# A recurrence's output bank: last part of the first four chunks behind the next chunk's first burst, and one ScalarE copy out of the bank

## The chip, the cores and the metric

The kernel runs on one core of a Trainium2 chip. The metric is the time of one execution in microseconds of the device. TensorE (PE) multiplies matrices into the accumulation banks (PSUM), VectorE (DVE), ScalarE (ACT) and GpSimd (POOL) work on tiles, SyncE (SP) issues most transfers. A bank holds 512 fp32 values for each of 128 partitions.

## The reference

One decoder layer for 2048 tokens of width 1024. The normed input is projected once and the result cut into three branches, each with a gate: a sliding-window attention, a cross-attention into 256 memory tokens, and a recurrence with a state matrix for each of 8 heads of width 64. The change touches only the recurrence:

```python
def rwkv7_scan(r, w, k, v, a, b):
    def step(S, inp):
        r_t, w_t, k_t, v_t, a_t, b_t = inp
        sa = jnp.einsum('bhvk,bhk->bhv', S, a_t)
        S = S * w_t[:, :, None, :] + sa[..., None] * b_t[:, :, None, :] + v_t[..., None] * k_t[:, :, None, :]
        y = jnp.einsum('bhvk,bhk->bhv', S, r_t)
        return S, y
...
    y = rwkv7_scan(rh, heads(decay), kh, vh, -kk, kk * ah)
    mean = jnp.mean(y, axis=-1, keepdims=True)
    var = jnp.mean(jnp.square(y - mean), axis=-1, keepdims=True)
    y = ((y - mean) * lax.rsqrt(var + LNX_EPS)).reshape(bsz, t, RW_WIDTH) * lnx_g.astype(f32) + lnx_b.astype(f32)
```

The three gated branches are projected, merged and added to the input.

## The kernel before

The tokens are worked through in four blocks of 512. In a block two streams are written side by side: `stream_r`, the recurrence, and `stream_f`, the two attentions and their projections. A projection (`proj`, through `gemm3`, L457 to L459) is 24 dense matmuls of 128x512 in the rounded fp32 format, since each operand is split into a high and a low part. Its result lies in one of two banks called mm, from which ACT or DVE takes it; `silu2` (L927 a tanh on ACT, L928 a product on DVE) is such a reader.

The recurrence takes its eight heads as four pairs, and the pairs in two groups of two. For a group, `rwkv_prep` makes the scaled keys and queries of all chunks of 64 tokens (QE and QO; AB; BK: L728 to L743 on DVE, L753 and L770 on PE, where L770 transposes BK), `rwkv_inverse` inverts a triangular matrix for each chunk, and `rwkv_chain` goes through the eight chunks in order. So a block has two chains, and the kernel eight. For chunk `c` a chain runs these bursts, four small fp32 matmuls each (two for S), each of which the profile shows as two passes:

- W (L866): state and values into a bank, copied to SBUF by DVE (L869).
- the w-part (L867): the chunk's first part of the output, into the bank `yps`. It reads what W reads.
- U (L874): the inverse times W; DVE multiplies the result into Z (L878, two products).
- the u-part (L859, `from_u`): the second part of the output. It needs the products of L878. For chunk `c` it is written behind U of chunk `c+1`, but for the chunks 3 and 7 into a burst of its own (L886).
- S (L881): the state's update; DVE adds it (L882) to the decayed state that ACT prepared (L872), and the next W needs that.

W and the w-part work on tiles of 128x64, U and the u-part on 64x64, S on the full 128x128.

The bank `yps` exists once and holds the output of four chunks, so a chain fills it twice. After chunk 3 and after chunk 7 DVE reads the bank: a sum over each head (L889), its mean (L890), and two subtractions into SBUF (L894). Only then may the w-part of chunk 4 open the bank again. Behind the chain come the variance (L900 on ACT, L902 on DVE), the scaling (L907) and four transposes (L910).

The order of instructions on each engine is not that of the program: `order` hands the whole program to a list scheduler (`steps`, `lay_out`) which goes by modelled durations (`cost_PE`, `cost_DVE` and so on) and by ranks, and the result is pinned for each engine. `burst` makes its matmuls one group that starts when all its operands are there (`together`); `behind` only fixes an order on PE. What a step of the recurrence waits for, PE fills with dense matmuls of projections. The temporary tiles of the recurrence come from `tmp`, six in turn.

Of the kernel before, what the change touches and what calls it, by code (L numbers as in the profile page):

```python
# [9 lines left out]
F32 = mybir.dt.float32  # L10
# [17 lines left out]
C = 64  # L28
NC_ = TB // C
# [268 lines left out]
def build(tc, A, nsb=4):  # L298
# [27 lines left out]
    def rw_ps():  # L326
        return ps.tile([128, 512], F32, name="rw", bufs=2)
# [509 lines left out]
    def rwkv_chain(group, Z, dk, hT, yas):  # L837
# [6 lines left out]
        def burst(ms, prev=None, after=()):  # L844
            together(ms)
            for m in ms:
                for u in after:
                    behind(m, u, True)
                if prev:
                    behind(m, prev)  # L850
                after, prev = (), m
            return prev
# [7 lines left out]

        upds = []
        for c in range(NC_):
            if c % per == 0:
                yps = y_ps().rearrange("p (i t e v) -> p i t e v", i=n, t=per // 2, e=2)
            pw = rw_ps()[:, :n * C].rearrange("p (i t) -> p i t", i=n)
            prev = burst([PE.matmul(pw[h, i], g[1][e][:, c, :C], Z[:, i, e, c], start=True, stop=True) for i, e, h, g in HH], None, upds)  # L866
            burst([PE.matmul(yslot(i, c, e), g[1][e][:, c, C:], Z[:, i, e, c], start=i == 0 and c % per == 0, stop=False) for i, e, h, g in HH], prev)  # L867
            W = rp.tile([128, n, C], F32, name="W", bufs=1)
            V.tensor_copy(W, pw)  # L869
# [5 lines left out]
            if c % per:  # L875
                prev = burst(from_u(c - 1), prev)
# [8 lines left out]
            if c % per == per - 1:  # L885
                burst(from_u(c), prev, upds[:1])  # L886

                mean = xp.tile([128, 8], F32, name="st8", bufs=2)
                V.tensor_reduce(mean, yps.rearrange("p i t e v -> p (i t e) v"), axis=AX.X, op=ALU.add)  # L889
                V.tensor_scalar(mean, mean, 1.0 / C, None, op0=ALU.mult)  # L890
                for i in range(n):
                    if c < per:
                        ycs.append(tmp())
                    V.tensor_tensor(chunks(ycs[i])[:, c // per * per:(c // per + 1) * per], yps[:, i].rearrange("p t e v -> p (t e) v"),  # L894
                                    mean[:, i * per:(i + 1) * per].unsqueeze(2).to_broadcast([128, per, C]), op=ALU.subtract)

# [482 lines left out]
```

## Time and profile before

| | |
|---|---|
| median of 3 runs | 2250.22 us (2249.85 to 2250.74) |
| the profiled execution | 2250.33 us |
| its span, first to last instruction | 2248.5 us |
| mean granted TensorE clock | 0.997 |
| dense matmuls of the projections on PE, `hH` and `hL` (L457 to L459) | 5664, 2248.0 us of overlapping durations |
| one dense matmul, duration in the record | 397 ns |

A matmul's duration in the record overlaps with that of the next, so its cost to PE is read from the distance of two starts. The rows of the timeline give start and length in us, engine, line, operation, what is written and what is read, and in brackets how long the engine sat idle before it and for whom. Groups of instructions give busy time in us and mean ns of one.

### The profile page before, as it was taken

To read this page: it belongs to the slowest core of one execution; us is meant where nothing else is said; L and a number is where in the kernel's file an instruction comes from. 1 tells how busy PE (TensorE), PEld (TensorE's weight loads), DVE (VectorE), ACT (ScalarE), POOL (GpSimd) and SP (SyncE) were. 2 spreads that over 40 slices of the span, in tenths; PEclk is the share of its full clock that TensorE was granted. 3 is DMA by queue.
4 is the path that set the end of the run, shared out by engine and by line. 5 is a ranking of instruction groups with operands and counts; after the bars stand their busy time and mean duration, and the time that the engine had idled before them with its cause. 6 is when DMAs were issued, how large, how long until landed. Compare 5 with 4: busy or idle time off the path is not lost.

```text
span 2248.5 us, 36875 instructions
## 1 busy us (share of the span) xinstructions
PE 2219.2 (99%) x13706; PEld 1806.1 (80%) x13706; DVE 1533.0 (68%) x3951; ACT 926.2 (41%) x2024; POOL 147.9 (7%) x209
## 2 busy tenths in 40 slices
PE   8999999999999999999999999999999999999999
PEld 7888778778888778878888878787888887787887
DVE  7799789775469777953437957985245895896312
ACT  6664565455253354423214345442223435434210
POOL 1000110000000011000000001000000001100000
PEclk9999999999999999999999999999999999999999
DMA  7777546679844444446774434445676444343655
GB/s 230 265 234 241 195 164 226 231 264 356 323 146 161 134 141 149 147 166 234 241 239 136 164 122 150 148 136 194 229 252 198 157 141 160 117 146 132 206 192 192
DMA packets 146226, 430.55 MB, mean 191 GB/s; under 512 B 16640, under 2 KB 21120, under 8 KB 146048
## 3 DMA queue, kind: packets, MB, share of 16 engines
q1 hardware_dynamic: 129920, 398.83, 52.6%
q10 hardware_dynamic: 16128, 29.37, 4.0%
q8 instruction: 109, 1.79, 0.3%
q14 instruction: 69, 0.57, 0.1%
HBM read 333.24 MB, written 94.90 MB: 190 GB/s over the span
## 4 chain that ended last, share of the span: by engine, by line
PE 74%; DVE 18%; ACT 3%; DMA 2%; issue 2%; POOL 1%; SPq 0%; DVEq 0%; ACTq 0%; POOLq 0%
PE mm L457 18%; PE mm L459 18%; PE mm L458 18%; DVE ibc L803 1%; PE rw L881 1%; DVE ibc L804 1%; ACT g L1102 1%; DVE Yi L805 1%; PE mm L1172 1%; PE mm L1174 1%; PE mm L1173 1%; PE oo L1003 1%; PE rw L866 1%; PE rw L874 1%; DVE g L1114 1%
## 5 line engine op out<-in xcount | busy, mean ns | idle before, releaser
L457 PE MATMUL mm<-hH,whl 128*128 128x512 f32 x1888 | 750.4, 397 | 5.8 <-DVE g L928 3.5
L459 PE MATMUL mm<-hH,whl 128*128 128x512 f32 x1888 | 748.9, 397 | 0.0
L458 PE MATMUL mm<-hL,whl 128*128 128x512 f32 x1888 | 748.7, 397 | 0.0
L457 PEld LDWEIGHTS mm<-hH,whl 128*128 128x128 f32 x1888 | 355.1, 188 | 77.9 <-DVE g L928 3.9
L459 PEld LDWEIGHTS mm<-hH,whl 128*128 128x128 f32 x1888 | 355.3, 188 | 69.4
L458 PEld LDWEIGHTS mm<-hL,whl 128*128 128x128 f32 x1888 | 355.3, 188 | 68.3 <-issue 0.7
L439 ACT ACTIVATE whl<-raw 128x512 fp32r<-128x512 f32 x178 | 111.2, 629 | 146.9 <-PE mm L459 80.1
L440 DVE TENSOR_TENSOR whl<-raw,whl 128x512 fp32r<-128x512 f32 x178 | 124.5, 702 | 50.6 <-ACT whl L439 49.5
L457 PE MATMUL mm<-yh,whl 128*128 128x512 f32 x384 | 151.3, 394 | 0.0
L458 PE MATMUL mm<-yl,whl 128*128 128x512 f32 x384 | 150.8, 393 | 0.0
L459 PE MATMUL mm<-yh,whl 128*128 128x512 f32 x384 | 150.7, 393 | 0.0
L872 ACT ACTIVATE SP<-Z,Pl 64x64 f32<-64x64 f32 x256 | 88.3, 345 | 115.0 <-DVE Z L882 111.4
L803 DVE STREAM_SHUFFLE ibc<-Nc 128x496 f32<-128x496 f32 (+30 forms) x248 | 113.4, 473 | 0.1
L1155 DVE SCALAR_TENSOR_TENSOR g<-g,mm 128x512 f32<-128x512 f32 x32 | 21.8, 681 | 128.6 <-PE mm L459 128.5
L804 DVE TENSOR_TENSOR ibc<-ibc,Yi 128x496 f32<-128x496 f32 (+30 forms) x248 | 104.5, 421 | 3.9
L805 DVE TENSOR_TENSOR Yi<-Yi,ibc 128x496 f32<-128x496 f32 (+30 forms) x248 | 103.2, 416 | 0.9
L882 DVE SCALAR_TENSOR_TENSOR Z<-rw,Pl,SP 64x64 f32<-64x64 f32 x224 | 63.5, 284 | 51.1 <-PE rw L881 47.5
L1140 ACT ACTIVATE gt<-mm 128x512 f32<-128x512 f32 x64 | 38.0, 593 | 144.1 <-PE mm L459 143.8
L457 PEld LDWEIGHTS mm<-yh,whl 128*128 128x128 f32 x384 | 72.1, 188 | 15.0 <-DVE g L1155 0.4
L459 PEld LDWEIGHTS mm<-yh,whl 128*128 128x128 f32 x384 | 72.1, 188 | 14.6
L458 PEld LDWEIGHTS mm<-yl,whl 128*128 128x128 f32 x384 | 72.1, 188 | 14.3
L1102 ACT ACTIVATE g<-g,mxs,st 128x256 f32<-128x256 f32 (+1 forms) x128 | 74.5, 584 | 18.4 <-DVE mxs L1095 18.2
(1902 smaller groups left out, 3783.9 us busy)
## 6 DMA issues: line engine op xcount, KB each, us to landing
whl<-k SPq DMA_DIRECT2D x486, 512.0 KB, 3.3
k<-whl SPq DMA_DIRECT2D x162, 512.0 KB, 4.4
raw<-in_w_in SPq DMA_DIRECT2D x118, 256.0 KB, 3.3
g<-in_x ACTq DMA_DIRECT2D x32, 256.0 KB, 4.4
out<-g ACTq DMA_DIRECT2D x32, 256.0 KB, 4.5
raw<-in_w_proj SPq DMA_DIRECT2D x24, 256.0 KB, 3.1
rt<-in_x ACTq DMA_DIRECT2D x24, 256.0 KB, 5.7
rt<-in_xt ACTq DMA_DIRECT2D x24, 256.0 KB, 5.8
```

The source lines that it names most:

```text
L439: S.activation(w[:, 0], raw, AF.Copy)
L440: V.tensor_tensor(w[:, 1], raw, w[:, 0].bitcast(F32), op=ALU.subtract)
L457: PE.matmul(out, lh, rh, start=i == 0, stop=False)
L458: PE.matmul(out, lh, rl, start=False, stop=False)
L459: PE.matmul(out, ll, rh, start=False, stop=i == n - 1)
L803: V.stream_shuffle(bc[:, :, :w], N_[:, :, s + 1:], [s] * 32)
L804: V.tensor_tensor(bc[:, :, :w], bc[:, :, :w], Y[:, :, s:s + 1].to_broadcast([128, n, w]), op=ALU.mult)
L805: V.tensor_tensor(Y[:, :, s + 1:], Y[:, :, s + 1:], bc[:, :, :w], op=ALU.add)
L872: S.activation(SP[h, i], Z[h, i, e, c], AF.Copy, scale=g[4][h, c:c + 1])
L882: upds = [V.scalar_tensor_tensor(Sst[h, g[0]] if c == NC_ - 1 else Z[h, i, e, c + 1], pS[h, i, e], g[4][h, c:c + 1], SP[h, i], op0=ALU.mul ...
L1102: S.activation(prs[b][:, i, m0:], prs[b][:, i, m0:], AF.Exp, scale=r2[:, b, i:i + 1], bias=mx[:, b, i:i + 1], accum_out=mx[:, b, 2 + i:3 + i])
L1140: S.activation(t, gp, AF.Tanh, scale=0.5)
```

## The change

The bank is taken out by one copy of ACT into a temporary tile (`take_y`, L868 of the new kernel); sum, mean and subtractions read that tile (L871 to L876), and one more tile of six is in use meanwhile. The u-part of chunk 3 is written behind W of chunk 4 (a burst of its own no more), the bank is emptied there, and the w-part of chunk 4 (`from_w`, L863) is written behind U of chunk 4, in the place where other chunks have a u-part; S stands behind it. The chain's end has the copy as well, with its u-part where it was. Nothing else is edited, but the scheduler lays out the program anew.

```diff
@@ -858,21 +858,47 @@
 
             return [PE.matmul(yslot(i, c, e), g[2][h, c, C:], Z[h, i, e, c], start=False, stop=i == n - 1 and c % per == per - 1) for i, e, h, g in HH]
 
+        def from_w(c):
+
+            return [PE.matmul(yslot(i, c, e), g[1][e][:, c, C:], Z[:, i, e, c], start=i == 0 and c % per == 0, stop=False) for i, e, h, g in HH]
+
+        def take_y(last):
+
+            full = tmp()
+            S.activation(full, yps.rearrange("p i t e v -> p (i t e v)"), AF.Copy)
+            part = full.rearrange("p (i s v) -> p i s v", i=n, v=C)
+            mean = xp.tile([128, 8], F32, name="st8", bufs=2)
+            V.tensor_reduce(mean, part.rearrange("p i s v -> p (i s) v"), axis=AX.X, op=ALU.add)
+            V.tensor_scalar(mean, mean, 1.0 / C, None, op0=ALU.mult)
+            for i in range(n):
+                if last < per:
+                    ycs.append(tmp())
+                V.tensor_tensor(chunks(ycs[i])[:, last // per * per:(last // per + 1) * per], part[:, i],
+                                mean[:, i * per:(i + 1) * per].unsqueeze(2).to_broadcast([128, per, C]), op=ALU.subtract)
+
         upds = []
         for c in range(NC_):
+            later = c % per == 0 and c
+            pw = rw_ps()[:, :n * C].rearrange("p (i t) -> p i t", i=n)
+            prev = burst([PE.matmul(pw[h, i], g[1][e][:, c, :C], Z[:, i, e, c], start=True, stop=True) for i, e, h, g in HH], None, upds)
+            if later:
+                burst(from_u(c - 1), prev)
+            W = rp.tile([128, n, C], F32, name="W", bufs=1)
+            V.tensor_copy(W, pw)
+            if later:
+                take_y(c - 1)
             if c % per == 0:
                 yps = y_ps().rearrange("p (i t e v) -> p i t e v", i=n, t=per // 2, e=2)
-            pw = rw_ps()[:, :n * C].rearrange("p (i t) -> p i t", i=n)
-            prev = burst([PE.matmul(pw[h, i], g[1][e][:, c, :C], Z[:, i, e, c], start=True, stop=True) for i, e, h, g in HH], None, upds)
-            burst([PE.matmul(yslot(i, c, e), g[1][e][:, c, C:], Z[:, i, e, c], start=i == 0 and c % per == 0, stop=False) for i, e, h, g in HH], prev)
-            W = rp.tile([128, n, C], F32, name="W", bufs=1)
-            V.tensor_copy(W, pw)
+            if not later:
+                burst(from_w(c), prev)
             SP = rp.tile([128, n, C], F32, name="SP", bufs=1)
             for i, e, h, g in HH:
                 S.activation(SP[h, i], Z[h, i, e, c], AF.Copy, scale=g[4][h, c:c + 1])
             pu = rw_ps()[:, :n * C].rearrange("p (i t) -> p i t", i=n)
             prev = burst([PE.matmul(pu[h, i], g[2][h, c, :C], W[h, i], start=True, stop=True) for i, e, h, g in HH])
-            if c % per:
+            if later:
+                prev = burst(from_w(c), prev)
+            elif c:
                 prev = burst(from_u(c - 1), prev)
             for e, h in ((0, EV), (1, OD)):
                 upd = V.tensor_tensor(Z[h, :n, e, c], pu[h], dk[h, :n, c:c + 1].to_broadcast([64, n, C]), op=ALU.mult)
@@ -882,18 +908,8 @@
             upds = [V.scalar_tensor_tensor(Sst[h, g[0]] if c == NC_ - 1 else Z[h, i, e, c + 1], pS[h, i, e], g[4][h, c:c + 1], SP[h, i], op0=ALU.mult, op1=ALU.add)
                     for i, e, h, g in HH]
             yield 4.247
-            if c % per == per - 1:
-                burst(from_u(c), prev, upds[:1])
-
-                mean = xp.tile([128, 8], F32, name="st8", bufs=2)
-                V.tensor_reduce(mean, yps.rearrange("p i t e v -> p (i t e) v"), axis=AX.X, op=ALU.add)
-                V.tensor_scalar(mean, mean, 1.0 / C, None, op0=ALU.mult)
-                for i in range(n):
-                    if c < per:
-                        ycs.append(tmp())
-                    V.tensor_tensor(chunks(ycs[i])[:, c // per * per:(c // per + 1) * per], yps[:, i].rearrange("p t e v -> p (t e) v"),
-                                    mean[:, i * per:(i + 1) * per].unsqueeze(2).to_broadcast([128, per, C]), op=ALU.subtract)
-
+        burst(from_u(NC_ - 1), prev, upds[:1])
+        take_y(NC_ - 1)
 
         for (p, _, _, _, _, yt), yc in zip(group, ycs):
             ysq = tmp()
```

Three places of the order. The first is PE at the boundary between the fourth and the fifth chunk, second group of the second block (mm are projections, rw the banks of W and U). Before, where the u-part of the fourth chunk stands alone two dense matmuls ahead of these rows, and four dense ones and S follow them:

```order
L866 MATMUL rw<-Z,QE 64x64
L866 MATMUL rw<-Z,QO 64x64
L866 MATMUL rw<-Z,whl 64x64 x2
L459 MATMUL mm<-hH,whl 128x512
L457 MATMUL mm<-yh,whl 128x512
L458 MATMUL mm<-yl,whl 128x512
L459 MATMUL mm<-yh,whl 128x512
L874 MATMUL rw<-W,AB 64x64 x2
L874 MATMUL rw<-W,whl 64x64 x2
L867 MATMUL yps<-Z,QE 64x64
L867 MATMUL yps<-Z,QO 64x64
L867 MATMUL yps<-Z,whl 64x64 x2
```

And after, where seven dense matmuls are ahead of the rows, and six and S follow (L883 is W, L859 the u-part, L898 U, L863 the w-part):

```order
L883 MATMUL rw<-Z,QE 64x64
L883 MATMUL rw<-Z,QO 64x64
L883 MATMUL rw<-Z,whl 64x64 x2
L859 MATMUL yps<-Z,AB 64x64 x2
L859 MATMUL yps<-Z,whl 64x64 x2
L457 MATMUL mm<-yh,whl 128x512
L898 MATMUL rw<-W,AB 64x64 x2
L898 MATMUL rw<-W,whl 64x64 x2
L458 MATMUL mm<-yl,whl 128x512
L863 MATMUL yps<-Z,QE 64x64
L863 MATMUL yps<-Z,QO 64x64
L863 MATMUL yps<-Z,whl 64x64 x2
```

The u-part joined W, and the w-part left U: one dense matmul now stands between them. In the first group of a block it is two.

The second place is PE in the same block's second preparation, where the keys BK are transposed into a bank of rw. Before:

```order
L457 MATMUL mm<-hH,whl 128x512
L458 MATMUL mm<-hL,whl 128x512
L770 MATMUL rw<-c_ident,BK 128x128 x4
L459 MATMUL mm<-hH,whl 128x512
L770 MATMUL rw<-c_ident,BK 128x128 x4
```

After:

```order
L459 MATMUL mm<-hH,whl 128x512
L457 MATMUL mm<-hH,whl 128x512
L770 MATMUL rw<-c_ident,BK 128x128 x8
L458 MATMUL mm<-hL,whl 128x512
L459 MATMUL mm<-hH,whl 128x512
```

Two stretches of transposes became one.

The third place is DVE in the first block, in the preparation of the second group, just behind the first chain's end. A projection's matmul on PE waits for the silu product there (L928, and L944 after), since it opens the bank that the product reads. Before:

```order
L728 SCALAR_TENSOR_TENSOR QO<-rt,Pt 64x8x64
L730 SCALAR_TENSOR_TENSOR rt<-rt 128x512
L735 TENSOR_TENSOR rk__2989<-rk__2989,rt 128x512
L440 TENSOR_TENSOR whl<-raw,whl 128x512
L732 TENSOR_TENSOR BK<-rt 64x8x64
L742 TENSOR_TENSOR QE<-rr__3114,Pt 64x8x64
L732 TENSOR_TENSOR BK<-rt 64x8x64
L440 TENSOR_TENSOR whl<-raw,whl 128x512
L928 SCALAR_TENSOR_TENSOR g_3505<-g_3505,mm 128x512
L737 TENSOR_TENSOR BK<-rk__2989,rt 64x8x64 x2
L742 TENSOR_TENSOR QO<-rr__3114,Pt 64x8x64
```

After:

```order
L730 SCALAR_TENSOR_TENSOR rt<-rt 128x512
L735 TENSOR_TENSOR rk__2993<-rk__2993,rt 128x512
L732 TENSOR_TENSOR BK<-rt 64x8x64
L440 TENSOR_TENSOR whl<-raw,whl 128x512
L732 TENSOR_TENSOR BK<-rt 64x8x64
L737 TENSOR_TENSOR BK<-rk__2993,rt 64x8x64 x2
L742 TENSOR_TENSOR QE<-rr__3118,Pt 64x8x64
L440 TENSOR_TENSOR whl<-raw,whl 128x512
L944 SCALAR_TENSOR_TENSOR g_3509<-g_3509,mm 128x512
L742 TENSOR_TENSOR QO<-rr__3118,Pt 64x8x64
```

The two products of L737 moved from behind the silu product to ahead of it. An instruction of the window attention (the one of L1094, three rows behind the silu product before) moved ahead of it too, further up.

## Prediction

> **What bounds the kernel now.** I read the engine table first, then the chain of work that ended last, then what TensorE (PE) waited for.
>
> ```profile
> PE 2219.2 (99%) x13706; PEld 1806.1 (80%) x13706; DVE 1533.0 (68%) x3951; ACT 926.2 (41%) x2024; POOL 147.9 (7%) x209
> PE 74%; DVE 18%; ACT 3%; DMA 2%; issue 2%; POOL 1%; SPq 0%; DVEq 0%; ACTq 0%; POOLq 0%
> PE mm L457 <- DVE g L928: 3.5, 1, 3.5
> PE rw L866 <- DVE Z L882: 2.4, 4, 1.4
> PE rw L881 <- DVE Z L878: 1.1, 3, 0.4
> ```
>
> PE has work for 99% of the span and carries 74% of the chain; it has almost always a projection to run while the recurrence waits for VectorE (DVE). So an edit pays in two ways only: by what PE itself spends, or by one of the few waits in the last three rows (us in total, times, longest). A shorter or longer recurrence by itself is worth nothing while projections fill the gap. The profiled execution took 2250.33 us (span 2248.5, 1.8 outside it), against a median of 2250.22; I sum against 2250.33 and take off 0.1 at the end.
>
> What a small burst costs PE is read around the boundary between the fourth and the fifth chunk, here that of the second group in the second block of tokens. I call the bursts by their lines: W (L866), its y part (L867, "w-part"), U (L874), the part from u (L859, "u-part") and S (L881). Between them stand dense 128x512 matmuls.
>
> ```profile
> 972.73 0.39 PE L459 MATMUL mm<-hH,whl 128*128 128x512 f32 x1
> ...
> 974.10 0.39 PE L459 MATMUL mm<-hH,whl 128*128 128x512 f32 x1
> 974.42 0.27 PE L866 MATMUL rw<-Z,QE 128*64 128x64 f32 x1
> ...
> 975.37 0.40 PE L458 MATMUL mm<-hL,whl 128*128 128x512 f32 x1
> 975.69 0.33 PE L874 MATMUL rw<-W,AB 64*64 64x64 f32 x4
> ...
> 976.64 0.39 PE L457 MATMUL mm<-hH,whl 128*128 128x512 f32 x1
> ```
>
> Six dense matmuls take 974.10 - 972.73 = 1.37, so 0.228 each. I count a stretch of small matmuls as the time from the start of the dense one before it to the start of the second dense one behind it, less two times 0.228: that takes in the slower slots on both sides. W with its w-part: 975.37 - 974.10 - 0.46 = 0.81. U with the u-part: 976.64 - 975.37 - 0.46 = 0.81.
>
> ```profile
> 978.23 0.40 PE L459 MATMUL mm<-hH,whl 128*128 128x512 f32 x1
> 978.56 0.33 PE L859 MATMUL yps<-Z,AB 64*64 64x64 f32 x4
> ...
> 979.27 0.40 PE L458 MATMUL mm<-hL,whl 128*128 128x512 f32 x1
> 979.60 0.27 PE L866 MATMUL rw<-Z,QE 128*64 128x64 f32 x1
> ...
> 980.32 0.39 PE L457 MATMUL mm<-yh,whl 128*128 128x512 f32 x1
> ...
> 980.79 0.39 PE L459 MATMUL mm<-yh,whl 128*128 128x512 f32 x1
> 981.11 0.33 PE L874 MATMUL rw<-W,AB 64*64 64x64 f32 x4
> ...
> 982.20 0.39 PE L458 MATMUL mm<-yl,whl 128*128 128x512 f32 x1
> ```
>
> The u-part alone: 979.27 - 978.23 - 0.46 = 0.58. W alone: 980.32 - 979.27 - 0.46 = 0.59. U with the w-part behind it: 982.20 - 980.79 - 0.46 = 0.95. So joining two bursts of one tile shape saves 0.58 + 0.58 - 0.81 = 0.35, and joining two of unlike shapes (64x64 and 128x64) saves 1.17 - 0.95 = 0.22. None of these rows shows a wait: PE loses nothing to this boundary now but the stretches.
>
> **The change, part by part.** *The boundary itself.* The u-part of the fourth chunk loses its stretch and rides behind W. But the fifth chunk's w-part now needs the copy of ScalarE (ACT), and in the order it no longer stands directly behind U: one or two dense matmuls come between. Before: u-part 0.58, W 0.59, U with w-part 0.95, in all 2.12. After: W with u-part, unlike shapes, 0.95; U alone 0.58, as the u-part alone, the same shape; w-part alone 0.59, as W alone; in all 2.12. So the ride saves **nothing** at seven of the eight boundaries. At the eighth (second group of the first block) all four stood apart before, 2.34, so 0.22 is saved.
>
> *The order elsewhere.* The list scheduler lays out the rest anew. Counted over both orders, PE's stretches of other than dense matmuls fall from 489 to 478: by two in the first block, by three in each other one; the pair of transposes in front.md is one. At 0.22 to 0.35 each that is 2.4 to 3.9 us. When I give every neighbouring pair in both orders the median slot that such neighbours have in the trace, the sum falls by 2.7, near the lower row. I take **-2.7**.
>
> *The copies.* Sixteen copies of a full bank are added on ACT, and the reduce and the subtracts read SBUF.
>
> ```profile
> L1140 ACT ACTIVATE gt<-mm 128x512 f32<-128x512 f32 x64 | 38.0, 593 | 144.1 <-PE mm L459 143.8
> L894 DVE TENSOR_TENSOR rt<-yps,st 128x256 f32<-128x256 f32 x32 | 12.8, 420 | 0.5
> L902 DVE TENSOR_REDUCE var<-rt 128x8 f32<-128x512 f32 x16 | 10.6, 682 | 2.3 <-ACT rt L900 2.2
> L890 DVE TENSOR_SCALAR st<-st 128x8 f32<-128x8 f32 x16 | 2.7, 168 | 0.4
> L878 DVE TENSOR_TENSOR Z<-rw,dk 64x128 f32<-64x128 f32 x128 | 36.8, 288 | 48.9 <-PE rw L874 36.7 <-ACT SP L872 5.6 <-PE yps L867 4.8
> L1070 DVE COPY st<-dh 64x4 f32<-64x4 f32 x48 | 8.3, 172 | 0.7
> ```
>
> A copy of that size is 0.59 on ACT, 9.5 us in all on an engine that works 41% of the time: no cost of its own. A reduce of this size from SBUF is 0.68 already, so DVE gains little; I take 0. The end of each chain gets 0.6 longer; dense matmuls hide it, except in the first block, below.
>
> *The new waits at the boundary.* S of the fifth chunk stands behind its w-part and behind the two products of L878, which in DVE's order now stand among the subtracts. From the start of W, first group: W with u-part about 0.9, copy 0.59, reduce 0.68, scalar 0.17, two L1070 copies 0.34, two subtracts 0.84, two products 0.58: about 4.1 us. PE meanwhile has the three stretches (2.12) and ten dense matmuls (2.28) less about 0.1 at the edge: S at 4.3. Second group: one subtract and no L1070 ahead of the last product, 3.4, against eight dense matmuls, 3.8. So it is covered, by 0.2 and 0.4. Were the cover gone, PE stands still with all that is queued behind S, DVE's state updates wait for S, and the next W for these. Bounds: 0, and 0.9 a boundary (one more 128x512 instruction of DVE, 0.68, and 0.2 on ACT), 7.2 for eight. I take 0, since each row in the sum is there, and keep 7.2 for a rival.
>
> *The first block's backlog on DVE.* After the first group's last chunk of the first block, DVE is busy without a gap and PE catches up with it:
>
> ```profile
> 295.87 0.39 PE L459 MATMUL mm<-hH,whl 128*128 128x512 f32 x1
> 299.76 0.53 PE L457 MATMUL mm<-hH,whl 128*128 128x512 f32 x1 [3.50 <-DVE g L928]
> ...
> 311.03 0.47 PE L457 MATMUL mm<-hH,whl 128*128 128x512 f32 x1 [0.83 <-DVE rk__3443 L660]
> L737 DVE TENSOR_TENSOR BK<-rk__2989,rt x2: 676/683/690, 299.6 to 300.3; 64x512 f32<-64x512 f32 x2
> 288.00:296.00 8.00, 8.00 (x41) 6.62 (x39) 7.83 (x19) 3.12 (x5) 1.54 (x1) 1.00 0.50 172
> 300.09:303.50 3.41, 3.41 (x9) 2.31 (x7) 2.86 (x8) 0.99 (x3) 0.00 (x0) 0.50 0.72 238
> ```
>
> The last two rows are stretches of time: length, busy time of PE, PEld, DVE, ACT and POOL, granted clock, DMA. DVE works 7.83 of 8 us ahead of the wait; for 3.41 us behind it PE has half its clock. The order now puts the two L737 (0.68 each) and a 0.17 ahead of the instruction that PE waits for: the wait grows by 1.5. It also swallows what PE saved before it in this block, 0.6 of the 2.7. In return DVE has that much less left behind it, and the 0.83 further on should go. So 1.5 + 0.6 - 0.8 = **+1.3**, with bounds 0 and 2.9 (the 0.8 does not come back, and one more 0.68 of DVE idles behind the copy). The half clock I leave as it is.
>
> What the Trainium skill says stands by itself: "TensorE: Matmul & The Clock Gate" (What's actually happening) has PE's clock halved after about one idle window of 3.4 us and released after a busy one. The trace agrees, with 3.50 idle and then 3.41 at 0.50. By that rule the longer wait costs the same one window, as in my sum; a wait well below it would give the half clock back, the third rival.
>
> **Sum:** -2.7 + 1.3 = -1.4: 2248.9 for the profiled execution, 2248.8 for the median. Its own range, from -3.9 + 0 to -2.4 + 2.9, is 2246.3 to 2250.7.
>
> **Rivals.** (1) *The chains' short waits go as well.* PE's waits for L882 and L878 (2.4 and 1.1 above) lie a chunk or two behind these boundaries, where the order changes too. Against it: those DVE instructions still queue with the same neighbours. If all go: -1.4 - 3.5 = -4.9, **2245.3**. Chance 0.12. (2) *S waits at the boundary*, the slower one. Place: S of the fifth chunk, eight times; price 0.9 each; it decides as soon as DVE or ACT holds more than the 0.2 to 0.4 of cover in that window. For it: the cover is thin in the first groups, and the other engines' timing is less regular than PE's. Against: whatever is in the order there is already in the sum. -1.4 + 7.2 gives **2256.0**; with the four first groups alone, 3.6, 2252.4. Chance 0.14. (3) *The backlog falls under the window.* If DVE starts its work after that chain earlier, the 3.5 us go, and with them half of 3.41: 2250.2 - 2.1 - 5.2 = **2242.9**. Against it: two instructions more stand ahead. Chance 0.04. That the change does not do what it says is not a rival: the order shows the ride and the copy at all eight places. The forecast keeps 0.70.
>
> **How the numbers follow.** A measurement of this kernel can tell about 0.2%, 4.5 us, from no change, so "same" is 2245.7 to 2254.7. Faster by more: rivals 3 and most of 1, and a little of the forecast's tail, 0.15. Slower by more: rival 2 with its full price, 0.10. Same: 0.75, with the forecast, a part of 1 and the milder half of 2. The range takes the forecast's own range, goes down to most of rival 1 and up to the milder half of rival 2: 2245.0 to 2252.8.
>
> **What would show it.** Right: at the boundary, stretches of 0.95, 0.58 and 0.59, no wait ahead of S, W's u-part or the w-part; near 296 us a wait of PE for the silu product (L944 now) of about 5 us and half clock behind it; the reduce still at 0.68; busy PE lower by two to three us. Wrong: waits for the products (L904) or for the copy (L868) in PE's list; a wait near 296 under 3 us; joined stretches dearer than 0.95.

## The result, and the profile after

The changed kernel takes 2255.74 us (median of 11 runs, 2254.39 to 2258.55), against 2250.9 for the kernel before on the same chip (11 runs): a ratio of 1.0024 with a 95% interval of 1.0016 to 1.0031. It is **slower by about 5 us** (0.2%), outside the predicted range of 2245.0 to 2252.8. The profiled execution has a span of 2253.6 us (2248.5 before). Its engine table:

```profile
PE 2219.0 (98%) x13706; PEld 1806.7 (80%) x13706; DVE 1535.0 (68%) x3951; ACT 932.6 (41%) x2038; POOL 152.2 (7%) x209
```

PE's busy time as a whole is that of before (2219.2), but by two differences that cancel: PE is busy for 1.7 us less in the start of the program, where it stands still for 2.1 more, and for 1.4 more in the first block, where more of it runs at half clock. Where the time goes has to be read stretch by stretch. What PE waited for, after (us in total, times, longest), leaving out the start of the program:

```profile
PE mm L457 <- DVE g L944: 4.5, 1, 4.5
...
PE rw L883 <- DVE Z L908: 2.8, 5, 0.8
PE rw L926 <- DVE rt L923: 2.6, 5, 0.7
PE rw L785 <- DVE carry L661: 2.5, 3, 0.8
...
PE rw L753 <- DVE QO L742: 2.1, 3, 0.7
...
PE mm L457 <- ACT gt L1156: 1.1, 1, 1.1
...
PE as__9413 L511 <- DVE g L509: 0.6, 1, 0.6
```

And rows of before at the same places (those of W and S are in the prediction):

```profile
PE rw L770 <- DVE whl L761: 2.5, 4, 1.1
...
PE rw L770 <- DVE QE L761: 2.1, 3, 0.7
...
PE rw L785 <- DVE carry L661: 1.0, 3, 0.3
...
PE rw L910 <- DVE rt L907: 0.4, 1, 0.4
```

Waits come in threes because the second to fourth block have the same order: the masked matmuls (L753) now wait, and the transposes of BK (L770) do so no more; the transposes behind a chain (L926) and those of v (L785) wait longer. The waits of the second block, in us:

| PE waits at | before | after |
|---|---|---|
| W | 0.31 | 0.52 |
| S | 0.36 | |
| the transposes behind a chain (L926) | | 0.44 |
| the masked matmuls (L753) | | 0.69 |
| the transposes of BK, two places | 0.69, 0.46 | |
| the window attention (L1128) | 0.34 | |
| a sum of squares (L511) | | 0.61 |
| the transposes of v (L785) | 0.33 | 0.83 |
| in all | 2.5 | 3.1 |

So the masked matmuls wait as long as the transposes of BK did before them, and that adds nothing; the other rows differ. None of these waits stands in the bursts of the boundary that the change is about. The nearest is W of the sixth chunk in the first block's first group, 0.78: VectorE's update of the fifth chunk's state (L908) stands there behind a row of the window attention that waits for GpSimd:

```profile
254.46 0.17 DVE L1110 SCALAR_TENSOR_TENSOR mxs<-mxs,st 128x8 f32<-128x8 f32 x1 [0.78 <-POOL st L426]
```

To see where the time goes I use that every kernel here has the same 8110 dense matmuls in almost the same succession (at most 216 places differ): the start of the n-th one, against that of the n-th one before, is how late PE is there. Cut by their number, the first block is the stretch from the 600th to the 1900th (166 to 555 us of before), and the chains and preparations of the others are 2500th to 3900th, 4500th to 5900th and 6500th to 7900th. The gaps in PE's rows give the idle time in each. After minus before, in us:

| | first block | second | third | fourth |
|---|---|---|---|---|
| time of the stretch | +3.05 | +0.51 | +1.15 | +0.67 |
| of it idle time of PE | +1.68 | +0.58 | +0.61 | +0.56 |

Between these stretches nothing moves by more than 0.2; 0.3 came up in the start of the program, where single executions differ by up to 1.9 us, and 0.3 went again behind the last stretch.

### The profile page after: what moved, and what is told of

Read it like the earlier page. It is cut to its first block, busy times and chain, and to the rows that moved or that the text cites. A ratio compares the mean times of both kernels' runs of the same rounds, so it can differ in the third digit from the quotient of the medians.

```text
span 2253.6 us, 36892 instructions
## 1 busy us (share of the span) xinstructions
PE 2219.0 (98%) x13706; PEld 1806.7 (80%) x13706; DVE 1535.0 (68%) x3951; ACT 932.6 (41%) x2038; POOL 152.2 (7%) x209
## 4 chain that ended last, share of the span: by engine, by line
PE 73%; DVE 17%; ACT 4%; DMA 2%; issue 2%; POOL 2%; SPq 0%; DVEq 0%; ACTq 0%; POOLq 0%
PE mm L457 18%; PE mm L458 18%; PE mm L459 18%; DVE ibc L803 1%; ACT g L1118 1%; PE mm L1188 1%; PE mm L1190 1%; PE mm L1189 1%; PE oo L1019 1%; PE rw L907 1%; DVE ibc L804 1%; DVE Yi L805 1%; PE oo L1144 1%; PE rw L883 1%; DVE g L1130 1%
## 5 line engine op out<-in xcount | busy, mean ns | idle before, releaser
L457 PE MATMUL mm<-hH,whl 128*128 128x512 f32 x1888 | 749.5, 397 | 6.1 <-DVE g L944 4.5
L457 PEld LDWEIGHTS mm<-hH,whl 128*128 128x128 f32 x1888 | 355.1, 188 | 76.5 <-DVE g L944 5.0
L457 PE MATMUL mm<-yh,whl 128*128 128x512 f32 x384 | 151.6, 395 | 1.2 <-ACT gt L1156 1.1
L908 DVE SCALAR_TENSOR_TENSOR Z<-rw,Pl,SP 64x64 f32<-64x64 f32 x224 | 63.5, 283 | 45.3 <-PE rw L907 41.9
L1156 ACT ACTIVATE gt<-mm 128x512 f32<-128x512 f32 x64 | 37.8, 591 | 117.7 <-PE mm L459 117.5
L457 PEld LDWEIGHTS mm<-yh,whl 128*128 128x128 f32 x384 | 72.1, 188 | 16.3 <-ACT gt L1156 1.2
```

The source lines that it names most:

```text
L457: PE.matmul(out, lh, rh, start=i == 0, stop=False)
L908: upds = [V.scalar_tensor_tensor(Sst[h, g[0]] if c == NC_ - 1 else Z[h, i, e, c + 1], pS[h, i, e], g[4][h, c:c + 1], SP[h, i], op0=ALU.mul ...
L1156: S.activation(t, gp, AF.Tanh, scale=0.5)
```

## The experiments

Each kernel was timed in five rounds beside the kernel before on the same chip (lines of edited kernels are shifted by the rows put in). An interval of such a median is about 2 us to either side, which is coarse here; the table above, made again for each run's profile, resolves 0.1 us in the idle time of the second to fourth block, but for a wait of 0.2 to 0.6 at a block's very end that comes and goes among executions (0.37 in e1's third block, 0.57 in e9's second). The first block is far less sure: with one and the same order there, PE's wait behind the second chain, near 486 us, is 0.4 to 0.8 in before, e1 and e9, and 0.6, 0, 1.8, 0 and 0 in the change, e2, e10, e12 and e13. A profile is of one execution, too: that of e4 took 5.2 us more than the run's median, those of e5 and e8 1.4 and 3.5 less. First all runs, less the kernel before:

| run | median, us | ratio, 95% interval | first block: time, idle, us at half clock | idle, blocks 2, 3, 4 |
|---|---|---|---|---|
| the change | +4.8 | 1.0016 to 1.0031 | +3.05, +1.68, 6.83 | +0.58 +0.61 +0.56 |
| e1 first block as before | +2.6 | 1.0000 to 1.0018 | +1.70, +0.40, 6.83 | +0.49 +0.80 +0.55 |
| e2 first block only | +3.5 | 1.0006 to 1.0024 | +1.56, +1.04, 3.41 | -0.01 -0.04 -0.06 |
| e3 ride, no copy | +2.2 | 1.0002 to 1.0019 | +2.72, +1.31, 6.83 | -0.62 -0.78 -0.64 |
| e4 copy, no ride | +0.4 | 0.9995 to 1.0012 | +4.98, +1.72, 10.24 | +0.07 -0.34 -0.28 |
| e5 silu product earlier | +4.8 | 1.0014 to 1.0034 | +1.72, +0.46, 6.83 | +0.53 +0.46 +0.46 |
| e6 before, silu later | +1.2 | 0.9995 to 1.0013 | +2.21, +1.69, 6.83 | +0.03 -0.07 0.00 |
| e7 no copy at the end | +3.4 | 1.0005 to 1.0023 | +3.33, +1.68, 6.83 | +0.07 +0.26 +0.06 |
| e8 w-part behind S | +3.9 | 1.0007 to 1.0025 | +3.87, +3.24, 6.83 | -0.85 -0.72 -0.87 |
| e9 before, end copy alone | +0.5 | 0.9993 to 1.0011 | +1.21, +0.15, 6.83 | +0.71 -0.04 +0.12 |
| e10 chain end earlier | +4.6 | 1.0011 to 1.0029 | +4.72, +2.90, 6.83 | +0.31 +0.28 +0.32 |
| e11 ride in later blocks | -2.7 | 0.9981 to 0.9999 | +0.21, -0.26, 3.41 | -0.66 -0.68 -0.58 |
| e12 tail moved forward | +4.8 | 1.0013 to 1.0032 | +2.67, +1.15, 6.83 | +0.37 +0.37 +0.44 |
| e13 and ScalarE's rows | +3.1 | 1.0008 to 1.0027 | +2.91, +1.13, 6.83 | +0.26 +0.17 +0.26 |

(Before: 3.41 us at half clock in the first block.)

**Where: the first block apart from the others (e1, e2).** The parts of the change get switches in `rwkv_chain`, which is given the block's number; with all three off it is the kernel before, row by row.

```diff
+        ride, copy_mid, copy_end = sb > 0, sb > 0, sb > 0
...
-            later = c % per == 0 and c
+            later = ride and c % per == 0 and c
...
-            full = tmp()
+            part = yps.rearrange("p i t e v -> p i (t e) v")
+            if copy_end if last == NC_ - 1 else copy_mid:
+                full = tmp()
...
+            if c == NC_ - 1 or c % per == per - 1 and not ride:
+                burst(from_u(c), prev, upds[:1])
+                take_y(c)
```

In e2 the three read `sb == 0`.

> Change in the second to fourth block alone; the first block is written as before. Theory A (the loss sits in the first block: the wait for the silu product of VectorE behind the first chain, 4.5 us, and two half-clock windows instead of one): the time is before plus 2 us at most (three blocks at about 0.7), and the first block shows the wait of 3.5 us and one window of 3.4 us at half clock again. Theory B (S waits at each fifth chunk's boundary, rival 2 of the prediction, spread over eight places): six of eight boundaries are left, so plus 3.8 of the 5 us. Theory C (the scheduler's new order costs wherever it differs): plus 3 to 5, since three of four blocks are laid out anew.

> The reverse: the change in the first block alone. Theory A: plus 3 to 4 us, the wait of about 4.5 us for the silu product near 300 us and about 6.8 us at half clock behind it. Theory B: two of eight boundaries, plus 1.2 us. Theory C: plus 1 to 1.5.

The two parts add up within their intervals: +2.6 and +3.5 against +4.8 for the whole, and in the profiles the waits are those of the whole change on one side of the cut and those of before on the other. So theory A, that the first block carries it, explains the larger part at best, and theory C's 1 to 1.5 for the first block is too small. Theory B (S waits at the boundary) falls: in neither profile does S of a fifth chunk wait at all.

The edited kernels keep parts of one order or the other row by row, so more profiles bear on this. In the first block those with the order of before (before, e1, and e9 but for its copies) take 0, +1.70 and +1.21 us, those with the order of the change (the change, e2, e10, e12, e13) +3.05, +1.56, +4.72, +2.67 and +2.91: on average 2.0 apart, of it 1.4 in idle time. For the three later blocks together the profiles with the order of before (before, e2, e6) and with that of the change (the change, e1, e5) lie 2.4 apart.

**Which edit (e3, e4).** In e3 VectorE reads the bank itself; e4 keeps the copy at both places and has the bursts where they were before.

```diff
-        ride, copy_mid, copy_end = True, True, True
+        ride, copy_mid, copy_end = True, False, False
```

e4 has `False, True, True`.

> The ride and the moved w-part, but VectorE reads the bank directly as before (no copy of ScalarE). Here the order of VectorE in the first block has the silu product ahead of the two L737 and of one L732. Theory A: no loss in the first block, the wait for the silu product at 3.5 us or under, one half-clock window at most; the time is before plus or minus 1. Theory B: S waits for the products behind reduce and subtracts: plus 3 to 5. If the ride is worth something of its own, minus 1 to 3.

> The copy of ScalarE at both places, bursts as before (u-part of the fourth chunk alone, w-part behind W). VectorE's order in the first block has the two L737 ahead of the silu product, as in the whole change. Theory A: the wait of 4.5 us or more and two half-clock windows, plus 3 to 5 us, about the whole loss. Theory B: nothing at the boundary, plus 0 to 1.

Each edit alone lowers the idle time of the later blocks, the ride by 0.6 to 0.8 each and the copy by 0.2 on average; together they raise it by 0.6. The effects do not add, which points to the order that the scheduler makes of each program, and not to an instruction that the change added; e9 below tests that with the order pinned. In the first block both show more idle time (+1.3 and +1.7), so theory A's clear case, the ride without a loss there, did not come.

**The first block's wait (e5, e6).** Here the pinned order is edited by hand, one instruction in VectorE's list, so that nothing else moves:

```diff
+    l = orders["DVE"]
+    i = next(i for i, s in enumerate(l) if s.writes[0][0] == "g2_3509" and any(r[4] for r in s.reads))
+    l.insert(i - 4, l.pop(i))
```

In e6 the same is done to the kernel before, with its silu product and `i + 2`.

> The whole change, with one edit to VectorE's order: in the first block the silu product that PE waits for is moved ahead of the two L737, one L742 and one weight product that stood ahead of it (2.5 us of VectorE). Theory A1 (that place is where the first block loses its 1.5 us beside the half clock): the wait falls from 4.5 to about 2.0 us, and the time comes down by 2 to 4 us against the whole change, to before plus 1 to 3. Rival A2 (VectorE is late as a whole there, so what is put behind is waited for next): the wait falls the same, another one of 1 to 2 us comes up within 10 us behind it, and the time stays at before plus 4 to 5. Blocks two to four must show the same waits as in the whole change, 0.5 to 0.6 us each over before.

> The kernel before, with its silu product in the first block put behind the two L737, as the change has it; nothing else. The prediction's term: the wait grows from 3.5 to 4.9 us, 0.8 of it comes back at the next wait, so plus 0.6 to 1.4. If a longer wait brings a second half-clock window by itself, 1.7 more: plus 2.3 to 3.1. If the number of half-clock windows depends on where the idle time falls among windows of 3.41 us, the profile may show one or two, and the median moves by 1 to 1.5.

PE's rows in e5, start and length, with the idle time before each in brackets:

```profile
298.08 0.39 PE L462 MATMUL mm<-hH,whl 128*128 128x512 f32 x1
300.54 0.71 PE L460 MATMUL mm<-hH,whl 128*128 128x512 f32 x1 [2.06 <-DVE g L947]
...
301.47 0.63 PE L462 MATMUL mm<-hH,whl 128*128 128x512 f32 x1
303.94 0.55 PE L756 MATMUL rw<-QO,BK 64*128 64x128 f32 x1 [1.84 <-DVE QO L745]
```

Of the 2.48 us that the wait lost, 1.84 came back three matmuls later, at QO, the product that stands behind the silu product in either order. This is what rival A2 forecast, and the median did not move. (The profile's first block has 1.2 us less idle time than the change's, but 0.6 of that is the wait near 486 us.) VectorE is late as a whole there, and its order only says which of PE's bursts waits. e6 gives the price of the prediction's own term by itself:

```profile
294.88 0.39 PE L462 MATMUL mm<-hH,whl 128*128 128x512 f32 x1
300.05 0.80 PE L460 MATMUL mm<-hH,whl 128*128 128x512 f32 x1 [4.78 <-DVE g L931]
```

3.50 became 4.78, +1.28; the 0.83 further on stayed at 0.81. With the second half-clock window in this execution the block is 2.2 us longer, and the median 1.2.

**The chain's end (e7, e9, e10).** e7 keeps the ride and the copy at the boundary, but VectorE reads the bank directly at the chain's end.

> Ride and copy at the boundary, but at the chain's end VectorE reads the bank directly as before. Theory D (the 0.6 us that each of the blocks two to four loses comes from the copy at the chain's end, which delays variance, transposes and what VectorE has next): PE's wait for L923's successor at the transposes (0.44 in each block) goes, and the idle time of PE in blocks two to four is back at that of before or under, so minus 1.8 us against the whole change. Rival E (it is the longer boundary: S comes 17 dense matmuls behind the S before it instead of 13): idle time of PE stays 0.5 to 0.6 us per block over before.

```diff
-        ride, copy_mid, copy_end = True, True, True
+        ride, copy_mid, copy_end = True, True, False
```

Idle time in the later blocks is back at that of before (+0.07, +0.26 with a wait of 0.30 at the block's very end, +0.06), as theory D said. But e7 is laid out anew too. e9 adds the copy at the chain ends to the kernel before and leaves every row of its order in place (the copies are put into `free`, and the scheduler is told that they take no time):

```diff
+        ride, copy_mid, copy_end = False, False, True
...
+        if ins.name in free:
+            s.dur = s.busy = s.lat = -45
```

> The kernel before with nothing but the copy of ScalarE at the eight chain ends; the scheduler is told that it costs nothing, so that every engine's order is the one of before, row by row. Theory D (0.6 us more at a chain's end are not hidden in blocks two to four): PE's idle time there grows by 0.3 to 0.6 us per block, the time by 1 to 2 us. The prediction's step (hidden by dense matmuls outside the first block): PE's idle time in blocks two to four within 0.1 us of before, the time within 1 us.

The chain then ends 0.46 us later (from the first W to the last subtract 48.34 instead of 47.88 in a first group), and PE's list of waits stays as it was:

```profile
PE mm L460 <- DVE g L951: 3.5, 1, 3.5
PE rw L773 <- DVE whl L764: 2.4, 4, 1.1
...
PE rw L892 <- DVE Z L914: 2.3, 4, 1.4
PE rw L773 <- DVE QE L764: 2.1, 3, 0.7
```

One wait of 0.1 at the transposes is new in each block. Theory D falls: of the 0.46, PE waits for 0.1 and the rest is hidden. In the whole change a first group's chain takes 48.90, 1.0 more than before, since its last u-part stands behind 32 matmuls of the window attention (2 us). e10 moves it and VectorE's reduce ahead of them.

> The whole change with two edits to the pinned order, in the first group of blocks two to four alone: the last u-part of the chain stands ahead of the 32 matmuls of the window attention instead of behind them (2 us), and VectorE's reduce, mean and subtracts ahead of the product that reads those matmuls. Theory D2 (what these blocks lose is the lateness of the first chain's end, since VectorE's in-order queue then idles for the variance and hands the next preparation's products over late): PE's waits for L923, L742 and L661 there (0.4, 0.7 and 0.8 us) shrink, idle time per block down by 0.4 to 0.7 us against the whole change, and a new wait of PE ahead of the u-part of at most 0.3. Rival G (the loss is in the order of the preparation itself): these waits stay within 0.1 us.

```diff
+    for i in range(1, len(l)):
+        if l[i].writes[0][0].startswith("yps") and any(r[0].startswith("Vt") for r in l[i - 1].reads):
+            j = next(j for j in range(i, 0, -1) if not l[j - 1].writes[0][0].startswith("oo"))
+            l[j:i + 4] = l[i:i + 4] + l[j:i]
```

The chain ends at 47.22, 1.7 earlier. Only the wait of 0.42 to 0.44 at the transposes goes, a new one of 0.14 stands ahead of the u-part, and the others stay: 0.78 at the masked matmuls, 0.82 at the transposes of v. So half of theory D2 is right, 0.3 of 0.6 us per block.

**What keeps VectorE late behind it (e12, e13).** e12 also puts ScalarE's second square and VectorE's second sum ahead of a shift, and PE's transposes four dense matmuls earlier; e13 puts ScalarE's rows behind the transposes in the order of before as well.

```diff
+            for k in (ty[0], ty[4]):
+                l[k - 4:k + 4] = l[k:k + 4] + l[k - 4:k]
...
+            take, a, other, x, y = l[k:k + 5]
+            b, c = (x, y) if x.writes[0][0] == a.writes[0][0] else (y, x)
+            l[k:k + 5] = a, b, other, take, c
```

> The kernel of the run e10, and in the same three places the rest of the chain's tail moved forward as well: ScalarE squares and VectorE sums the second tile ahead of the shift for the next preparation (as the order of before has it), and PE's two bursts of four transposes stand four dense matmuls earlier. Theory H (in blocks two to four the change loses at the place of these transposes in the pinned order: VectorE's first product for the next preparation waits 2.5 to 2.8 us for them, so the products that PE's masked matmuls need come 1.1 us later than in before): that idle time of VectorE shrinks by 0.8 to 1 us, PE's wait for L742 at the masked matmuls (0.69 to 0.78) goes or falls under 0.1, and idle time per block falls by 0.5 to 0.9 against the run e10, to before or under. Rival G (the order of the preparation itself): that wait stays at 0.6 or more. The first block is as in the whole change, and the whole time between before plus 1.5 and plus 3.5 us.

> The kernel of the run e12 with one more edit in the same three places: ScalarE finishes the first tile's scalings (L931 twice) and begins the second's before it takes a projection out of its bank, as in the order of before. Theory I (VectorE's first product waits for ScalarE behind that take-out): VectorE's 4.6 us of idle time fall to under 2.8, its later products come about 0.7 us earlier (then the rotation's shuffle waits for ScalarE), PE's wait at the masked matmuls falls from 0.86 to 0.90 to 0.1 to 0.3, and idle time per block by 0.5 to 0.7 us against e12, to 0.1 to 0.3 under before. Rival: the wait stays above 0.6, because another row gates VectorE; then the place stays open.

VectorE in e12 and then in e13, each at the first product behind the transposes and at the row that PE's masked matmuls wait for (by then the execution of e13 is 1.4 us later as a whole, so the first product came 2.6 earlier and the last row 0.4):

```profile
814.63 1.27 DVE L943 TENSOR_TENSOR rt<-rt,var 128x512 f32<-128x512 f32 x2
820.50 0.69 DVE L952 TENSOR_TENSOR ya<-ya,rt 128x512 f32<-128x512 f32 x1 [4.60 <-ACT rt L951]
...
834.93 0.69 DVE L762 TENSOR_TENSOR QO<-rr__8794,Pt 64x512 f32<-64x512 f32 x1
```

```profile
819.33 0.69 DVE L956 TENSOR_TENSOR ya<-ya,rt 128x512 f32<-128x512 f32 x1 [2.05 <-ACT rt L955]
...
821.90 0.01 DVE L597 LOAD_MASK_SELECT g<-g  x1 [1.14 <-ACT g L1095]
...
827.05 0.69 DVE L540 TENSOR_TENSOR rt<-rw,eye 128x512 f32<-128x512 f32 x1 [0.46 <-PE rw L535]
828.03 0.69 DVE L1192 SCALAR_TENSOR_TENSOR mB<-gt,mm 128x512 f32<-128x512 f32 x1 [0.29 <-PE mm L483]
...
835.94 0.69 DVE L766 TENSOR_TENSOR QO<-rr__8794,Pt 64x512 f32<-64x512 f32 x1
```

Theories H and I fall. What came earlier was waited for again, at the next row that needs ScalarE or PE (4.60, then 2.05 and 1.14, 0.46, 0.29), and in e13 PE still waits 0.69 for L766. VectorE's queue is paced by several rows of other engines in turn, and freeing the last of them uncovers the one before. **What stays open** is which rows of the layout make the remaining 0.2 to 0.4 us per block, among them the 0.5 more at the transposes of v: that wait is 0.8 in every profile with the order of the whole change there (e1, e5, e10, e12, e13), and 0.3 to 0.4 in e2, e3, e4, e7, e8, e9 and e11. The 0.6 at L511 stands in the same profiles as the 0.8, and no run tried either of them by itself.

**The boundary's own price (e8).** The w-part of chunk 4 is written behind S. Its operand rows have then been overwritten by the products, so this kernel leaves the first part of chunk 4's output to other values; its time is read for the wait alone.

```diff
-            if later:
-                prev = burst(from_w(c), prev)
-            elif c:
+            if c and not later:
...
+            if later:
+                prev = burst(from_w(c), prev)
```

> The whole change, but the w-part of the fifth chunk is written behind S, so S no longer stands behind the copy. Rival E: S of the fifth chunk comes 13 or 14 dense matmuls behind the fourth's as before, the chain ends 1 us earlier, idle time of PE in blocks two to four back at before, minus 1.8 us against the whole change. Theory D: idle time there as in the whole change. In the first block VectorE's order differs from both kernels (the silu product stands 12 rows further behind), so the first block may lose more; it is read apart.

S of chunk 4 comes 5.46 us behind that of chunk 3 instead of 6.48 (5.59 before), and the later blocks' idle time falls by 1.3 to 1.4 each against the whole change. This is the largest effect there, just above the 1.2 to 1.4 of taking out the copy (e3). It bears on a dependence that the prediction did not name: the products of L904 overwrite rows of Z that the w-part reads, so in the program they stand behind the w-part and with it behind the copy. No row of the profile waits for the w-part, though: as in the prediction, the products are held in VectorE's list, behind the reduce and a subtract. PE does not stand still for it, since the scheduler knew it and put four dense matmuls more between S and S; whatever it costs is paid in how the rest is laid out. That this is the cause is not shown by itself: e3 has 7.69 us there and loses nothing.

**A version that beats both (e11).** The first block is that of before with the silu product three rows earlier in VectorE's order; the later blocks ride without the copy.

```diff
+        ride, copy_mid, copy_end = sb > 0, False, False
...
+    l.insert(i - 3, l.pop(i))
```

> A version meant to beat both: the first block as in before but for its silu product, which VectorE makes three rows earlier; in blocks two to four the ride without the copy. From the runs with the ride alone: blocks two to four 0.4 to 0.6 us each less than before. In the first block the wait falls from 3.5 to about 2.2 us, and, as when the product was moved in the changed kernel, another wait of up to 1.8 us takes most of its place: 0 to 1 us less. In all before minus 1.5 to 2.5; if the moves only shift waits about, within 1 us of before.

2247.81 against 2250.50, a ratio of 0.9990 (0.9981 to 0.9999): faster by 2.7 us, just clear of the noise, of which the profile has 1.8 in the later blocks' times (0.59, 0.63 and 0.55). The first block's wait fell from 3.50 to 2.06, and the next one grew from 0.83 to 1.54, as in e5.

## Why the prediction was wrong, by its own steps

The forecast was -1.4 and the median moved by +4.8. Of these 6.2 us, 2.7 are the stretches that saved nothing, and about 2.4 are the later blocks, which the sum put at nothing (1.7 of it waits); the rest is the first block, +2.0 to +3.5 instead of +1.3.

**The stretches, -2.7: the step that failed first.** Their number did fall from 489 to 478. But I priced each one saved at 0.22 to 0.35, and that row belongs to bursts of small tiles. What joined were bursts on full 128x128 tiles: in each later block two of the three joins are transposes, the third is of window attention. Before, with a wait of 0.69 taken out, and after:

```profile
836.63 0.40 PE L458 MATMUL mm<-hL,whl 128*128 128x512 f32 x1
837.72 0.63 PE L770 MATMUL rw<-c_ident,BK 128*128 128x128 f32 x4 [0.69 <-DVE QE L761]
838.11 0.48 PE L459 MATMUL mm<-hH,whl 128*128 128x512 f32 x1
838.43 0.60 PE L770 MATMUL rw<-c_ident,BK 128*128 128x128 f32 x4
838.78 0.47 PE L457 MATMUL mm<-hH,whl 128*128 128x512 f32 x1
839.10 0.39 PE L458 MATMUL mm<-hL,whl 128*128 128x512 f32 x1
```

```profile
840.92 0.40 PE L457 MATMUL mm<-hH,whl 128*128 128x512 f32 x1
841.15 1.24 PE L770 MATMUL rw<-c_ident,BK 128*128 128x128 f32 x8
842.15 0.47 PE L458 MATMUL mm<-hL,whl 128*128 128x512 f32 x1
842.46 0.39 PE L459 MATMUL mm<-hH,whl 128*128 128x512 f32 x1
```

Two stretches: 839.10 - 836.63 - 0.69 - 3 x 0.228 = 1.10. One: 842.46 - 840.92 - 0.46 = 1.08. Joining saved 0.02. Summed over all stretches of a later block without their waits, PE spends 80.92, 80.95 and 80.48 us before and 80.97, 80.98 and 80.47 after: nothing was saved in any of them.

**The boundary, 2.12 before and after: right.** Its three stretches in the second group of the second block, after:

```profile
983.10 0.40 PE L459 MATMUL mm<-hH,whl 128*128 128x512 f32 x1
983.43 0.27 PE L883 MATMUL rw<-Z,QE 128*64 128x64 f32 x1
...
984.19 0.50 PE L457 MATMUL mm<-yh,whl 128*128 128x512 f32 x1
984.62 0.33 PE L898 MATMUL rw<-W,AB 64*64 64x64 f32 x4
...
985.00 0.50 PE L458 MATMUL mm<-yl,whl 128*128 128x512 f32 x1
985.43 0.27 PE L863 MATMUL yps<-Z,QE 128*64 128x64 f32 x1
...
985.81 0.50 PE L459 MATMUL mm<-yh,whl 128*128 128x512 f32 x1
986.15 0.39 PE L457 MATMUL mm<-yh,whl 128*128 128x512 f32 x1
```

From 983.10 to 986.15, less four dense slots of 0.228, are 2.14 us, against 2.12. No wait stands ahead of S, the u-part or the w-part there, and S stands 4.32 us behind W in that block's first group, where the prediction had 4.3: the second rival, 0.9 at each boundary, did not come. Of the first, S's waits shrank (L907 0.4, 1.1 before), but W's did not (L883 2.8, 2.4 before). The third did not come either.

**The first block, +1.3 with half clock "as it is": the path was wrong, the size less so.** The wait grew to 4.54, by 1.04 instead of 1.5. But PE was not 0.6 early at it, it was 3 us late. Of these, 0.9 are PE's own time, for as many stretches as before (46 between the 600th dense matmul and the wait), and 2.1 are waits that I had not looked for (L457 for ScalarE's L1156 1.05, W 0.78 and 0.43, the transposes L926 0.72, S 0.38 among them, against 1.44 and 0.12 before). Behind it 1.6 come back: the 0.83 is gone, and the 1.10 at L770 fell to 0.29. The idle time sums to +1.7. That the 2.0 us by which the two orders differ on average lie within the term's bounds of 0 to 2.9 (2.8 by what it names) is luck: they are made of other waits.

**The half clock, "the same one window": wrong, but not for the wait's length.** Windows of 3.41 us around the wait, with PE's busy time and the granted clock: the change, then e1 and e2 (columns as in the prediction).

```profile
299.02:302.43 3.41, 0.62 (x3) 0.19 (x1) 3.34 (x6) 1.23 (x2) 0.00 (x0) 1.00 0.92 296
302.43:305.85 3.42, 1.66 (x5) 0.92 (x5) 3.30 (x7) 0.70 (x3) 0.00 (x0) 0.50 0.69 228
305.85:309.26 3.41, 3.41 (x32) 3.40 (x32) 1.30 (x3) 3.41 (x13) 0.00 (x0) 0.50 0.41 166
```

```profile
298.70:302.11 3.41, 2.66 (x6) 2.15 (x7) 3.35 (x7) 0.00 (x0) 0.00 (x0) 0.50 0.91 312
302.11:305.53 3.42, 3.42 (x22) 2.60 (x22) 1.04 (x4) 2.90 (x10) 0.00 (x0) 0.50 0.09 35
```

```profile
303.43:306.84 3.41, 3.41 (x31) 3.22 (x32) 1.87 (x5) 3.22 (x11) 0.00 (x0) 0.50 0.57 208
```

e1 has the order and the wait (3.50) of before, and two windows where before has one; e2 has the order and the wait (4.56) of the change, and one. By the windows of their profiles e9, with the order of before, has two; so have e10, e12 and e13, with that of the change. Counting half of PE's busy time in them as lost, it is 1.7 us before, 2.5 in the change, 3.0 in e1, 1.7 in e2, and on average 2.5 with the order of before and 2.6 with that of the change. So the number differs among executions of one order; that it depends on where the idle time falls among the windows is my reading. Between the profiles of before and e1 it makes 1.3 us; it is no part of the change that could be read from an order. Nor does a shorter wait give the full clock back, as the third rival and the rule beside it had it: in e11 the wait is 2.06, PE is busy for 1.35 of the 3.41 us of that window, and a window at half clock follows all the same.

**"The end of each chain gets 0.6 longer; dense matmuls hide it": right for the copy (e9), wrong for the change.** The later blocks lose 0.6 each in idle time, from an order in which rows of VectorE come later against PE's fixed list: the scaling ahead of L926 (0.43 more), the shift ahead of the transposes of v (0.5 more) and the row ahead of L511, less what W, S, L1128 and the second transposes of BK waited before. The sum treated the new order as a rearrangement of costs that are read from the old one; the new layout has its own waits, and these were never estimated. Of before's list of waits the prediction read three rows; those of the preparations (the transposes of BK, 2.5 and 2.1, and of v, 1.0), two of them longer than a row that it read, were left out, and there the later blocks changed most. With e1 and e2 the loss is about 2.6 there and 3.5 in the first block, each give or take 2; by the profiles it is 2.4 and 2.0.

## What to carry to other kernels

Where a scheduler lays out a whole program again, a small edit costs what its new waits cost, and these do not follow from the edit: two edits that each lower the idle time can raise it together. Price the edit by itself with the order pinned (e6, e9), and read a new layout for its waits, engine by engine, before pricing what it saves. Moving up the last thing that an engine with a pinned order waits for gains only what the next wait leaves over: 0.64 of 2.48 us in e5. One profile of each kernel is little to go by: look which runs share a stretch of the order, and compare those.

## What the runs showed of the hardware

- Joining bursts on tiles of 64x64 or 128x64 saves 0.2 to 0.35 us of PE (the rows of the prediction), joining transposes of full 128x128 tiles 0.02.
- Waits that follow from the pinned order repeat within 0.1 us among executions and blocks (0.69 at the masked matmuls in all twelve cases of the change, e1, e5 and e13). The start of the program, the wait near 486 us and the half-clock windows do not: 1.9 us among the profiles of this study at the 600th dense matmul, 0 to 1.8 with one order at that wait, and one or two windows at the same wait of VectorE's silu product.
- PE's busy time in a window at half clock does not tell by itself whether the next one has full clock. A window with 2.82 of 3.41 us busy was followed by full clock in e3, one with 2.66 in e1 was not, and neither was one with 2.83 in e13. In e3:

```profile
300.29:303.70 3.41, 2.82 (x7) 2.24 (x8) 3.32 (x7) 0.00 (x0) 0.00 (x0) 0.50 0.76 245
303.70:307.12 3.42, 3.42 (x40) 2.78 (x38) 2.02 (x5) 2.96 (x10) 0.00 (x0) 1.00 0.08 29
```

And in e13:

```profile
303.95:307.36 3.41, 2.83 (x15) 2.08 (x17) 2.12 (x5) 1.87 (x7) 0.00 (x0) 0.50 0.74 256
307.36:310.77 3.41, 3.41 (x26) 3.07 (x25) 2.44 (x4) 2.78 (x10) 0.00 (x0) 0.50 0.06 25
```

The Trainium skill ("TensorE: Matmul & The Clock Gate", What's actually happening) speaks of a free-running window of activity. The traces agree in that half clock comes in whole windows of 3.41 us, one or two for the same wait of 3.50 (before and e1); how much of a window must be busy these rows leave open.
